# A list schedule over the recorded program in place of a scheduler with priorities, in a hybrid encoder block on one core

## The chip, the cores and the metric

The kernel runs on one core of one Trainium2 chip. The metric is device time in microseconds of one execution. A core has TensorE (matrix products into PSUM), VectorE (DVE), ScalarE (ACT), GpSimd (POOL) and SyncE (SP, which here only issues transfers). Each engine has a queue of its own that it works through in order; between engines there are semaphores, so an instruction at the head of a queue holds up everything behind it until what it needs is there.

## The reference, cut to what matters

One layer of an encoder: 512 positions, model width 1024, everything in float32.

```python
h = rmsnorm(x); proj = h @ w_in                      # 1024 -> 768 + 256 + 32 + 3*512
c_q, c_kv, k_pe, u_h = split(proj)
q = rmsnorm(c_q) @ w_uq; kv = rmsnorm(c_kv) @ w_ukv  # 8 heads, q/k of 64 + 32 (rotary), v of 64
q, k = rope(rmsnorm(q)), rope(rmsnorm([k_nope, k_pe]))
y_attn = softmax(q k^T / sqrt(96)) v                 # bidirectional
x0, x1, vh = split(dwconv3(u_h))
y_hyena = x0 * (fftconv(x1 * vh, filters) + bias * x1 * vh)   # filters: three sine layers, a decay
x = x + [rmsnorm(y_attn), rmsnorm(y_hyena)] @ w_out
up = dwconv3(rmsnorm(x) @ w_up); x = x + (silu(g) * u) @ w_down   # 2 x 2816
x = x + sigmoid(x @ w_gate) * rmsnorm(p @ w_ple)
```

## The kernel before, in words

Activations lie transposed: channels on the 128 partitions, the 512 positions along the free dimension. A float32 product is made of three products of rounded parts: every operand is split into a high part (a copy on ScalarE) and a low part (a subtraction on VectorE), and mms (L173, matmuls at L176) runs high x high, high x low, low x high. Weights come as 128 x 1024 tiles in one stream of their own order: next_w (L166) keeps the loads three tiles ahead, and wload (L137) makes a transfer into wr on SP, the high part wh on ScalarE (L142) and the low part wl on VectorE (L143), for half of many tiles by a transfer from GpSimd's queue that adds (L145, L146).

The stages in order of time are: the loads of x and its squares (accx, accy); the input projections, 21 tiles of 24 matmuls each (in_gemm, L313), of which the first three are the kv latents and the rotary key; the norm's scale R1 (rms_bcast, L218, and rsqrt, L203: a logarithm, an exponential and a Newton step on ScalarE and VectorE) with which every product is multiplied as it leaves PSUM (L509, L621); between them the Hyena filters (filter_task, three sine layers at L370 to L377) and the transforms of the Hyena input, as matmuls with a table dft; the products of the spectra on VectorE (L589 to L599) and their sums, split into Y (L610); the keys (wk) and the six query tiles in the order UQ; head sums of the squares by matmuls with sel, whose eight rows are copied by ScalarE (rows, L667), turned by four tiny transposes (turn_rows, L231) and made into scales (rms_cols); the list TAIL, in which inverse transforms (E, O), values (V), first scores (S) and a gate (G) stand; the attention, 8 heads of four row blocks each (scores, softmax, turn, weigh, finish), with the other gates (products at L833 to L835, square and sum at L841 and L842, then a split) and the Hyena part of the output product (hyena_out, residual add at L929) mixed in; the attention part of the output product; 44 up tiles with their convolution (conv, L536 to L543), silu and gate; the down product; the embedding; the last gate with sigmoid and the store.

PSUM has eight banks in two rings of four, mm (psm) and ax (psx). Temporaries of the first stages are ten rotating tiles (tmp, NTMP), x tiles are eight, weights three high, three low and two raw.

What sets the order of the work is this. TensorE's order is written out by hand: its matmuls are issued as the program text makes them. Side work of TensorE (filter, transforms, key, query scale) is written as generators that are woven into the projections by a clock: advance(cost) adds the cost in us of the matmuls just made, and spawn(task, delay) puts a task's next piece at clock + delay; these delays are the constants D_SIN, D_FILT, D_RMS and so on. All other engines are put in order by the framework's scheduler at build time: it goes by priorities, which follow the program order, changed by offsets in the table PRI and by high_priority blocks, and by its own estimate of the times. rope, ident and the dft tables are loaded by SP and GpSimd in the middle of this; the GpSimd ones are held behind the statistics by issue_after. L651 fixes one place at which ScalarE's exponential table is loaded.

Pools of tiles open and close with ExitStack: ft (first stages) closes at L893 before the attention's pools at and ap open in its place, and at, ap, hp and gp close before fp, the pool of the feed-forward stage.

## Time and profile before

| | |
|---|---|
| three runs, median (lowest to highest) | 759.44 us (757.58 to 759.54) |
| the profiled execution, its own time | 757.62 us |
| its span, from first to last instruction | 755.8 us |
| mean granted TensorE clock | 0.991 |
| TensorE busy | 723.0 us (96%), 3254 matmuls recorded |
| VectorE, ScalarE, GpSimd busy | 504.8, 373.1, 151.7 us |
| read from memory | 77.00 MB, 105 GB/s over the span |

A row of a timeline has the start in us, the busy time in us, the engine, the line, the operation, the tiles out<-in, the form and the count; in brackets stands the idle time of the engine before it and what ended it. A row of a wait says which instruction of which engine waited for which: us in total, times, longest. A granted clock below 1.00 in a stretch means that TensorE was throttled for part of it. A line can be a helper's: L176 is every matmul of mms, L131, L132, L134 and L135 are the two halves of split.

### The profile page before, as it was taken

What the parts mean: (1) busy time and instruction counts of PE and PEld (TensorE: products, weight loads), DVE (VectorE), ACT (ScalarE), POOL (GpSimd) and SP (SyncE); (2) the same over time, 40 slices, a digit from 0 to 9 for tenths busy, and PEclk for the clock granted to TensorE, in tenths of its full rate; (3) what the DMA queues carried; (4) which work ended last, traced back from release to release, by engine and by line L of the source; (5) the groups of instructions that cost most, each with busy time, mean ns of one, the idle gap of its engine ahead of it and who ended that gap; (6) DMA issues with size and microseconds to landing.
All of it is one profiled execution on the core that took longest, in us unless ns stands there. A gap on an engine that the chain in (4) does not pass through costs nothing.

```text
span 755.8 us, 9037 instructions
## 1 busy us (share of the span) xinstructions
PE 723.0 (96%) x3254; PEld 582.7 (77%) x3254; DVE 504.8 (67%) x780; ACT 373.1 (49%) x575; POOL 151.7 (20%) x150
## 2 busy tenths in 40 slices
PE   6999999996997899999999999999999999999997
PEld 4767888874665777788888888888888888888886
DVE  6499988888779987885766566666665332233482
ACT  7465545467668896564534444444353222126340
POOL 2111101110126662130422222222122000005000
PEclk9999999997999999999999999999999999999999
DMA  8765744443636210533232323232323233323331
GB/s 279 239 153 128 191 128 91 106 94 77 147 91 170 71 25 19 126 103 106 83 113 84 112 84 112 83 104 92 106 89 92 82 109 101 98 90 127 111 112 56
DMA packets 30110, 82.83 MB, mean 110 GB/s; under 512 B 3913, under 2 KB 5257, under 8 KB 30066
## 3 DMA queue, kind: packets, MB, share of 16 engines
q1 hardware_dynamic: 24418, 71.62, 31.2%
q0 software_dynamic: 5392, 10.25, 7.2%
q10 hardware_dynamic: 256, 0.39, 0.2%
q8 instruction: 25, 0.41, 0.2%
q14 instruction: 19, 0.16, 0.1%
HBM read 77.00 MB, written 2.10 MB: 105 GB/s over the span
## 4 chain that ended last, share of the span: by engine, by line
PE 54%; DVE 0%; ACT 0%; DVEq 0%; issue 0%
PE mm L176 37%; PE ax L176 17%; PE ax L220 0%; DVE t L1127 0%; ACT t L1126 0%; DVEq L1294 0%; DVE t L1128 0%
## 5 line engine op out<-in xcount | busy, mean ns | idle before, releaser
L176 PE MATMUL mm<-a,wh 128*128 128x512 f32 (+1 forms) x928 | 288.8, 392 | 9.2 <-ACT wh L273 6.4
L176 PEld LDWEIGHTS mm<-a,wh 128*128 128x128 f32 x928 | 174.3, 190 | 51.2 <-issue 6.5
L143 DVE TENSOR_TENSOR wl<-wr,wh 128x1024 fp32r<-128x1024 f32 (+3 forms) x113 | 124.3, 1101 | 113.8 <-ACT wh L142 111.8
L142 ACT ACTIVATE wh<-wr 128x1024 fp32r<-128x1024 f32 (+1 forms) x113 | 116.5, 1031 | 158.0 <-PE mm L176 121.6
L176 PE MATMUL mm<-a,wl 128*128 128x512 f32 (+1 forms) x464 | 180.7, 389 | 0.0
L176 PE MATMUL ax<-a,wh 128*128 128x512 f32 x384 | 118.3, 389 | 0.0
L176 PEld LDWEIGHTS mm<-a,wl 128*128 128x128 f32 x464 | 88.1, 190 | 17.8 <-DVE wl L274 0.2
L176 PEld LDWEIGHTS ax<-a,wh 128*128 128x128 f32 x384 | 72.1, 188 | 14.9
L176 PE MATMUL mm<-g,wh 128*128 128x512 f32 x232 | 73.8, 400 | 1.7 <-ACT t L647 1.7
L176 PE MATMUL ax<-a,wl 128*128 128x512 f32 x192 | 74.7, 389 | 0.0
L1063 POOL TENSOR_TENSOR f<-f 128x512 f32<-128x512 f32 x22 | 28.7, 1303 | 169.2 <-DVE f L543 149.5
L176 PE MATMUL mm<-h,wh 128*128 128x512 f32 x192 | 59.0, 389 | 0.0
L176 PEld LDWEIGHTS mm<-g,wh 128*128 128x128 f32 x232 | 44.2, 192 | 13.7 <-ACT t L647 2.1
L176 PE MATMUL mm<-g,wl 128*128 128x512 f32 x116 | 46.1, 397 | 0.0
L176 PEld LDWEIGHTS ax<-a,wl 128*128 128x128 f32 x192 | 36.0, 188 | 7.6
L176 PEld LDWEIGHTS mm<-h,wh 128*128 128x128 f32 x192 | 36.0, 188 | 7.5
L1059 DVE TENSOR_TENSOR f<-mm,R 128x512 f32<-128x512 f32 x22 | 15.2, 691 | 33.7 <-PE mm L176 33.7
L176 PE MATMUL mm<-h,wl 128*128 128x512 f32 x96 | 37.3, 389 | 0.0
L1062 ACT ACTIVATE f<-f 128x512 f32<-128x512 f32 x22 | 13.9, 631 | 44.8 <-DVE f L543 44.8
L536 ACT ACTIVATE f<-f,par 128x512 f32<-128x512 f32 x44 | 35.5, 808 | 1.0 <-DVE f L1059 1.0
L543 DVE SCALAR_TENSOR_TENSOR f<-f,par 128x511 f32<-128x511 f32 x44 | 33.9, 771 | 1.4
L146 POOL DMA_DIRECT2D wl<-in_w_in_dram x16 | 13.9, 868 | 103.8 <-DVE wl L143 53.5
(312 smaller groups left out, 1015.1 us busy)
## 6 DMA issues: line engine op xcount, KB each, us to landing
wr<-in_w_up_dram SPq DMA_DIRECT2D x44, 512.0 KB, 3.5
wr<-in_w_in_dram SPq DMA_DIRECT2D x19, 512.0 KB, 3.9
wr<-in_w_down_dram SPq DMA_DIRECT2D x16, 512.0 KB, 3.5
x<-in_xT_dram SPq DMA_DIRECT2D x16, 256.0 KB, 4.2
wl<-in_w_in_dram POOLq DMA_DIRECT2D x16, 256.0 KB, 5.3
wr<-in_w_out_dram SPq DMA_DIRECT2D x8, 512.0 KB, 4.4
wr<-in_w_gate_dram SPq DMA_DIRECT2D x8, 512.0 KB, 3.6
wr<-in_w_down_dram SPq DMA_DIRECT2D x8, 384.0 KB, 3.1
```

What stands on the lines that cost most here:

```text
L142: S.activation(hi[:, :n], raw[:, :n], AF.Copy)
L143: V.tensor_tensor(lo[:, :cut], raw[:, :cut], f32(hi[:, :cut]), op=ALU.subtract)
L146: G.dma_start(lo[:, cut:n], src[:, cut:n], accum_op=ALU.add)
L176: last = PE.matmul(out, l, r, start=start and i == 0, stop=stop and i == n - 1)
L536: S.activation(c, z, AF.Identity, scale=pcol(w, 3 * m + 1), bias=pcol(b, m))
L543: V.scalar_tensor_tensor(c[:, 0 : T - 1], z[:, 1:T], pcol(w, 3 * m + 2), c[:, 0 : T - 1], op0=ALU.mult, op1=ALU.add)
L1059: V.tensor_tensor(z, ps_up.pop(m), R2, op=ALU.mult)
L1062: S.activation(cc[0], cc[0], AF.Silu)
L1063: G.tensor_tensor(cc[1], cc[0], cc[1], op=ALU.mult)
```

## The change

The body of the kernel is nearly unchanged, but its engines are now recorders. Every call (matmul, activation, transfer) becomes an Op in a Plan, with the tiles and boxes that it reads and writes. Tiles become PlannedTile, whose buffer is chosen by the planner. At the end plan.issue() puts all ops in sequence and only then emits them, each engine's in the order found. The framework orders nothing any more (engines=None), and all high_priority blocks, PRI offsets and the fixed place of the table load are gone (issue preloads the exponential table wherever the plan changes back to it).

The order is found as follows. TensorE's ops get a due time each, by adding up their durations in recorded order from 5.5 us. Every other op is due in time for the earliest of its successors: that one's due time less its own duration and latency, for a transfer also 2 us and its bytes. Successors are found through data only (overlapping boxes of a tile). Then time is played through: of each engine's ready ops the one that can start first is taken, and among those within 0.02 us of it the one due first. TensorE's ops can therefore leave the recorded order. Tiles of one tag take buffers in recorded order, when one is free. Ops before a pool change (close) are all placed before any op after it. The durations come from a cost function; all but TensorE's and SP's are stretched by 1.05, and an operation of VectorE or GpSimd with `port` is not placed beside one of the other.

Further edits: the delays of the side tasks are new, with query_scale at 18.5 instead of 6.5 and the sine layers at 2.0 instead of 8.0; UQ is now 5, 2, 4, 3, 0, 1; KLAG goes from 3 to 2 and NRH, the block at which the Hyena norm is made, from 10 to 15. Of the entries in ENG three take effect: the residual adds of hyena_out (xt, L929) go from VectorE to GpSimd; the scaled sum in the Hyena norm (vh) goes from VectorE to ScalarE; the squares in rms_cols (sc) do so too. QACT goes from 1 to 0, so head 0's four transfers in prep (L745, L746) are issued by SP instead of ScalarE. rope and ident are now recorded as behind the statistics too, which only the plan sees.

```diff
@@ -23,37 +23,37 @@
 T_IN = 5.1
 T_UQ = 3.9
 T_K = 1.3
-D_SIN = 8.0
-D_FILT = 9.5
-D_TR = 5.0
-D_HALF = 7.0
-D_RMS = 6.5
+D_SIN = 2.0
+D_FILT = 13.5
+D_TR = 1.0
+D_HALF = 8.5
+D_RMS = 18.5
 D_LAT = 0.0
-D_UU = 13.5
-D_UT = 5.0
+D_UU = 13.0
+D_UT = 1.0
 D_MUL = 3.5
-D_SPR = 2.0
+D_SPR = 6.0
 D_SQ = 13.0
 NTMP = 10
 D_LR = 7.0
-D_KC = 2.5
-D_RC = 1.5
+D_KC = 4.5
+D_RC = 2.5
 W0N = 512
 W0B = 2
 W1A = 3
 W1B = 4
-KLAG = 3.0
-NRH = 10
-D_FT = 8.5
+KLAG = 2.0
+NRH = 15
+D_FT = 11.5
 TAIL = 'E0 P E1 R O S0 S1 V0 V1 S2 S3 V2 G0 V3'
...
-QACT = 1
-UQ = (2, 0, 4, 3, 5, 1)
-D_KS = 5.0
-D_KR = 4.5
-D_TAIL = 15.5
+QACT = 0
+UQ = [5, 2, 4, 3, 0, 1]
+D_KS = 6.0
+D_KR = 5.0
+D_TAIL = 16.5
...
+MARGIN = 0.1
+AIM = 0.0
+STRETCH = {'V': 1.05, 'S': 1.05, 'G': 1.05, 'PE': 1.0, 'SP': 1.0}
...
+    def cost(self, op):
+        a, kw = op.args, op.kw
+        out = a[0]
+        n = 1
+        for k in out.shape[1:]:
+            n *= k
+        op.table, op.byte, op.lat, op.port = None, 0, 0.2, False
+        if op.fn == "dma_start":
+            op.byte = 4 * n * out.shape[0]
+            op.dur = 0.6 if op.eng == "G" else 0.45
+            op.lat = 0.0
+            return
+        if op.eng == "PE":
+            if op.fn == "transpose":
+                op.dur = 0.11 if a[1].shape[0] > 8 else 0.07
+            elif a[1].dtype == F32:
+                op.dur = max(0.222, 0.855 * n / T) if n > 8 else 0.222
+            else:
+                op.dur = (n + 32) / 2400.0
+            op.lat = 0.25
+        elif op.eng == "V":
+            if op.fn == "reduce_max":
+                op.dur = 0.6
+            elif op.fn in ("tensor_tensor", "stream_shuffle"):
+                op.dur = 0.07 + n / 960.0
+            elif op.fn == "reciprocal":
+                op.dur = 0.1
+            elif op.fn == "tensor_scalar" and not any(isinstance(v, View) for v in a[2:]) and not a[1].tile.tag.pool.psum:
+                op.dur = 0.08 + n / 1900.0
+            else:
+                op.dur = 0.12 + n / 960.0
+            op.lat = 0.22
+            ins = [v for v in list(a[1:]) + list(kw.values()) if isinstance(v, View) and v.shape[1] * len(v.shape) > 16]
+            op.port = n > 64 and len(ins) > 1 and not any(v.tile.tag.pool.psum for v in ins)
+        elif op.eng == "S":
+            op.dur = 0.09 + n / 1190.0
+            if isinstance(kw.get("scale"), View) or isinstance(kw.get("bias"), View):
+                op.dur += 0.06
+            if kw.get("accum_out") is not None:
+                op.dur += 0.15
+            op.lat = 0.24
+            op.table = TABLES.get(a[2])
+        elif op.eng == "G":
+            op.dur = 0.05 + (n / 780.0 if op.fn == "tensor_scalar" else n / 410.0)
+            op.port = n > 64 and op.fn != "memset"
+        else:
+            op.dur = 0.1
+
+    def order(self):
+        clock = 5.5
+        for op in self.ops:
+            if op.eng == "PE":
+                op.due = clock
+                clock += op.dur
+            else:
+                op.due = None
+            for p in op.preds:
+                p.succs.append(op)
+        for op in reversed(self.ops):
+            need = clock + 50.0 if op.due is None else op.due
+            for s in op.succs:
+                need = min(need, s.due - op.dur - op.lat - AIM - (2.0 + op.byte / 2.0e5 if op.byte else 0.0))
+            op.due = need
+        engines = {e: 0.0 for e in self.handles}
+        port = {"V": 0.0, "G": 0.0}
+        table, moved, done = "exp", 0.0, []
+        begun = 0
+        for seg in range(len(self.cuts) + 1):
+            last = self.cuts[seg] if seg < len(self.cuts) else len(self.ops)
+            ops = self.ops[begun:last]
+            begun = last
+            ready = {e: [] for e in engines}
+            for op in ops:
+                op.wait = sum(1 for p in op.preds if p.end is None)
+                op.est = max([p.end for p in op.preds if p.end is not None], default=0.0)
+                if not op.wait:
+                    ready[op.eng].append(op)
+            left = len(ops)
+            while left:
+                best = None
+                for e, cand in ready.items():
+                    now, fit = None, []
+                    for op in cand:
+                        t = max(op.est, engines[e])
+                        if op.port:
+                            t = max(t, port["G" if e == "V" else "V"])
+                        ok = True
+                        for tile, _, _ in op.acc:
+                            if tile.slot is None:
+                                tag = tile.tag
+                                if tag.tiles[tag.next] is not tile:
+                                    ok = False
+                                    break
+                                slots = [s for s in tag.open_slots() if s.free is not None]
+                                if not slots:
+                                    ok = False
+                                    break
+                                t = max(t, min(s.free for s in slots))
+                        if ok:
+                            fit.append((t, op))
+                    if not fit:
+                        continue
+                    now = min(t for t, _ in fit)
+                    t, op = min(((t, op) for t, op in fit if t <= now + 0.02), key=lambda x: (x[1].due, x[1].i))
+                    if best is None or t < best[0]:
+                        best = (t, op)
+                assert best is not None, "no operation fits"
+                t, op = best
+                for tile, _, _ in op.acc:
+                    if tile.slot is None:
+                        tag = tile.tag
+                        slot = min((s for s in tag.slots if s.free is not None), key=lambda s: s.free)
+                        slot.free, tile.slot = None, slot
+                        tag.next += 1
+                dur = op.dur * STRETCH[op.eng]
+                if op.table is not None and op.table != table:
+                    dur += 1.28
+                    table = op.table
+                engines[op.eng] = t + dur
+                op.end = t + dur + op.lat
+                if op.port:
+                    port[op.eng] = t + dur
+                if op.byte:
+                    rate = 1.0e5 if op.kw.get("accum_op") is not None else 2.7e5
+                    moved = max(moved, t + dur) + op.byte / (2.7e5)
+                    op.end = max(moved, t + dur + op.byte / rate) + 2.0
+                for tile in {x[0] for x in op.acc}:
+                    tile.left -= 1
+                    tile.end = max(tile.end, op.end)
+                    if not tile.left:
+                        tile.slot.free = tile.end
+                ready[op.eng].remove(op)
+                for s in op.succs:
+                    if s.seg == seg:
+                        s.wait -= 1
+                        s.est = max(s.est, op.end + (MARGIN if s.eng != op.eng else -op.lat))
+                        if not s.wait:
+                            ready[s.eng].append(s)
+                done.append((t, op))
+                left -= 1
+        self.done = done
+        return done
+
...
+            real = lambda v: v.real() if isinstance(v, View) else v
+            getattr(self.handles[op.eng], op.fn)(*[real(v) for v in op.args], **{k: real(v) for k, v in op.kw.items()})
...
-    V, S, G, PE, SP = nc.vector, nc.scalar, nc.gpsimd, nc.tensor, nc.sync
+    plan = Plan(tc, {"V": nc.vector, "S": nc.scalar, "G": nc.gpsimd, "PE": nc.tensor, "SP": nc.sync})
+    V, S, G, PE, SP = (plan.engine(k) for k in ("V", "S", "G", "PE", "SP"))
...
-    ctx.enter_context(tc.manual_schedule(engines={mybir.EngineType.PE}))
+    ctx.enter_context(tc.manual_schedule(engines=None))
...
-    SP.dma_start(rope, c_rope)
-    SP.dma_start(ident, c_id)
-    with tc.issue_after(gate_consts.ins):
+    plan.behind = gate_consts
+    if True:
+        SP.dma_start(rope, c_rope)
+        SP.dma_start(ident, c_id)
...
-    p0.close()
...
+    plan.close(ft)
...
+    plan.issue()
```

More of the change, by code (lines that the diff above doesn't have):

```diff
@@ new lines, with __init__, open_slots, view @@
+class Slot:
+    def __init__(self, pool, tag, n):
+        self.pool, self.tag, self.n = pool, tag, n
+        self.free = 0.0
+class Tag:
+    def __init__(self, pool, name, bufs):
+        self.pool, self.name, self.bufs = pool, name, bufs
+        self.tiles, self.next, self.slots = [], 0, None
+    def open_slots(self):
+        if self.slots is None:
+            self.slots = [Slot(self.pool, self, n) for n in range(min(self.bufs, len(self.tiles)))]
+        return self.slots
+class PlannedTile:
+    def __init__(self, tag, shape, dtype):
+        self.tag, self.shape, self.dtype = tag, tuple(shape), dtype
+        self.width = 1
+        for n in shape[1:]:
+            self.width *= n
+        self.slot, self.left, self.first, self.end, self.real = None, 0, None, 0.0, None
+        self.log = []
+    def view(self):
+        return View(self, np.arange(self.shape[0] * self.width, dtype=np.int32).reshape(self.shape), (), self.dtype)
@@ new lines, with __init__, __getattr__ @@
+class Op:
+    __slots__ = ("i", "eng", "fn", "args", "kw", "acc", "seg", "preds", "succs", "dur", "lat", "due", "wait", "est", "new", "end", "table", "byte", "port")
+class Recorder:
+    def __init__(self, plan, eng, handle):
+        self._plan, self._eng, self._handle = plan, eng, handle
+    def __getattr__(self, fn):
+        return lambda *args, **kw: self._plan.record(self._eng, fn, args, kw)
+TABLES = {AF.Ln: "exp", AF.Exp: "exp", AF.Sin: "sin", AF.Silu: "silu", AF.Sigmoid: "sigmoid"}
@@ L162, in ahead @@
         while len(ready) < min(i, len(stream)):
-            with tc.high_priority(offset=WPRI if len(ready) > 3 else 0):
+            with nullcontext():
                 ready.append(wload(*stream[len(ready)]))
@@ L506, in tile_encoder_block @@
         G.memset(f32(t8), 0.0)
+    plan.behind = None
     ckv = [xpool.tile([P, T], F32, tag="x", name="x") for _ in range(2)]
```

190 lines of the change are left out of this document (163 added, 27 removed).

## The prediction

> **What bounds the kernel now.** I read the page first (engines, slices, chain), then the waits of TensorE alone, then stretches of the span cut where those waits lie, then the timelines around the longest ones.
>
> ```profile
> span 755.8 us, 9037 instructions
> PE 723.0 (96%) x3254; PEld 582.7 (77%) x3254; DVE 504.8 (67%) x780; ACT 373.1 (49%) x575; POOL 151.7 (20%) x150
> PE   6999999996997899999999999999999999999997
> PE 54%; DVE 0%; ACT 0%; DVEq 0%; issue 0%
> ```
>
> TensorE is busy 723.0 of 755.8 us, and the chain that ended last is TensorE for 54% of the span, some 408 us back from its last matmul near 751 us. The change removes no matmul, so the whole stake is TensorE's idle time of 32.8 us and the time in which its clock is low. Stretches (span, busy time and count of PE, PEld, DVE, ACT, POOL, then the granted clock, DMA share, GB/s) place both:
>
> ```profile
> 0.00:6.40 6.40, 0.00 (x0) 0.00 (x0) 0.76 (x2) 3.15 (x5) 0.45 (x6) 1.00 0.55 172
> 33.00:35.00 2.00, 0.14 (x2) 0.07 (x1) 1.93 (x4) 0.15 (x1) 0.00 (x0) 1.00 0.89 230
> 35.00:39.40 4.40, 4.40 (x13) 3.46 (x14) 2.83 (x6) 3.71 (x6) 0.88 (x1) 0.61 0.51 109
> 39.40:57.00 17.60, 16.71 (x65) 11.52 (x64) 16.59 (x28) 10.80 (x15) 1.73 (x2) 1.00 0.59 146
> 57.00:160.00 103.00, 103.00 (x460) 84.37 (x458) 93.02 (x159) 49.27 (x75) 12.97 (x15) 1.00 0.54 129
> 160.00:175.80 15.80, 14.15 (x59) 9.65 (x58) 13.18 (x23) 12.06 (x20) 2.60 (x3) 1.00 0.45 88
> 175.80:182.00 6.20, 0.43 (x5) 0.32 (x4) 6.20 (x12) 5.21 (x9) 0.00 (x0) 0.79 0.27 86
> 182.00:189.60 7.60, 7.58 (x18) 4.39 (x18) 4.84 (x14) 5.19 (x11) 0.86 (x1) 0.50 0.11 23
> 189.60:228.00 38.40, 36.14 (x161) 25.38 (x160) 28.51 (x67) 25.89 (x55) 7.90 (x9) 1.00 0.50 122
> 228.00:313.00 85.00, 76.69 (x437) 62.31 (x438) 75.47 (x164) 64.85 (x130) 42.73 (x47) 1.00 0.31 77
> 313.00:751.10 438.10, 437.63 (x1946) 361.53 (x1944) 243.38 (x285) 175.31 (x226) 75.35 (x57) 1.00 0.32 99
> 751.10:755.80 4.70, 0.00 (x0) 0.00 (x0) 1.43 (x4) 0.66 (x2) 0.00 (x0) 1.00 0.17 56
> ```
>
> Two pieces are out of reach: the first 6.4 us (the first loads) and the last 4.7 us (last sigmoid, two products, store). From 313 to 751.1 us only 0.47 us is idle. The remaining 21.2 us, 20.7 of it in the rows shown, lies before 313 us. To it comes slow matmul time: 4.4 us at clock 0.61 loses 4.4 x 0.39 = 1.7 us, 7.6 us at 0.50 loses 3.8 us. The pool is 21.2 + 5.5 = 26.7 us. Second thing to see: VectorE is busy 16.59 + 93.02 + 13.18 + 6.20 + 4.84 + 28.51 = 162.3 of the 188.6 us from 39.4 to 228 (86%) and 75.47 of 85 (89%) after it, so it is nearly a second bound there.
>
> The waits of TensorE (us in total, times, longest):
>
> ```profile
> PE ax L231 <- ACT t L667: 6.5, 2, 5.8
> PE ax L176 <- DVE ptl L132: 3.2, 2, 2.9
> PE mm L176 <- DVE x L509: 1.9, 1, 1.9
> PE mm L176 <- ACT t L647: 1.7, 1, 1.7
> PE ax L370 <- ACT x L377: 0.9, 1, 0.9
> ```
>
> **The change part by part.** The sum is made against the profiled execution: 757.62 us, 1.8 us around its span. Its runs have the median 759.44.
>
> **(1) The stall at 175.8 us.** Four tiny transposes of the query's row sums (L231) stand in TensorE's fixed order before the copy that feeds them (L667) is made. ScalarE's queue holds that copy behind splits that each wait for VectorE:
>
> ```profile
> 171.08 1.02 PE L674 MATMUL ax<-accx,ones 128*8 128x512 f32 x2
> 182.01 0.59 PE L231 MATMUL ax<-ident,t 8*128 8x8 f32 x4 [5.79 <-ACT t L667]
> 179.65 0.63 ACT L131 ACTIVATE a<-t 128x512 fp32r<-128x512 f32 x1 [0.58 <-DVE t L610]
> 181.39 0.57 ACT L667 ACTIVATE t<-ax 8x512 f32<-8x512 f32 x1
> ```
>
> The sums were done at 172.1, the copy started at 181.4. After the change query_scale is recorded 18.5 us of TensorE cost behind the keys instead of 6.5, so some 12 us of query matmuls go ahead of it; the copy inherits an early due time from the transposes; and the planner lets a ready matmul overtake one whose operand is late. Best case 5.79 + 3.8 = 9.6 us. Late next are the key's own row sums, which go through the same copy, and Y, the spectra whose sixteen VectorE operations (L610, L132) fill that queue. VectorE has 13.18 + 6.20 + 4.84 of 29.6 us filled, that is 24.2; with 9.6 us closed only 20.0 us are left, so 4.2 us of its work must slide on, into 189.6 to 228, where it has 9.9 us free. I take 8.0 (range 2 to 9.6).
>
> **(2) The stall at 33 us.** The fifth projection needs a PSUM bank that L509 frees, which needs R1, the input norm's scale:
>
> ```profile
> 27.54 2.24 ACT L142 ACTIVATE wh<-wr 128x1024 fp32r<-128x1024 f32 x2 [7.96 <-DMA wr<-in_w_in_dram]
> 30.20 0.67 ACT L205 ACTIVATE R<-ax,eps 128x512 f32<-128x512 f32 x1
> 34.12 1.29 DVE L509 TENSOR_TENSOR x<-mm,R 128x512 f32<-128x512 f32 x2
> ```
>
> ScalarE waited 7.96 us for a weight with the logarithm of R1 queued behind it. An order by due times could start it ahead of the two splits (2.24 us) and recover 1.9 + 1.7 = 3.6 us. But due times run through data, not through PSUM banks: freeing a bank gives no urgency, and the two weight splits keep theirs. Between 0 and 3.6 I take half, 1.8. The row at 35 us shows clock 0.61 after an idle time of 1.86 us. The Trainium skill (TensorE: Matmul & The Clock Gate, "Why this matters for your kernels") says to avoid idle gaps over some 3 us, since a window of idle halves the clock; by that rule this stall would cost 1.9 and its cure half of that; the trace here goes against the rule, since the shorter gap already halved the clock.
>
> **(3) Two small stalls,** 0.9 (third row of the small filter network waits for its sine) and 1.7 (a bank waits for the square at L647): greedy order of TensorE should fill about half, 1.3 of 2.6 (0 to 2.6).
>
> **(4) 189.6 to 228,** 2.26 us idle. Here the softmax scale is a chain of small operations, and pulling the rest of the stretch together uncovers it. Against it: the plan closes at each pool change (L893), so all operations recorded before the attention precede all later ones on every engine. Gate 0's split, now run at 234.12 amid the attention, must come before the first probabilities; that is one VectorE operation of 0.76 us. Net 0.8 (-1 to 2.3).
>
> **(5) The attention, 228 to 313,** 8.3 us idle, VectorE at 89%. The longest stall follows one operation:
>
> ```profile
> 234.12 2.94 DVE L135 SCALAR_TENSOR_TENSOR a<-x,par,a 128x512 fp32r<-128x512 f32 x1
> 242.75 0.76 DVE L135 SCALAR_TENSOR_TENSOR a<-x,par,a 128x512 fp32r<-128x512 f32 x1
> 233.92 1.36 POOL L869 TENSOR_SCALAR pr<-pr,st 128x512 f32<-128x512 f32 x2
> 235.25 1.26 POOL L842 TENSOR_TENSOR x<-x,t 128x512 f32<-128x512 f32 x1
> 238.01 0.68 DVE L132 TENSOR_TENSOR ptl<-ax,pth 128x512 fp32r<-128x512 f32 x1
> 238.84 0.93 PE L176 MATMUL ax<-ks,qs 96*128 96x512 f32 x3 [2.93 <-DVE ptl L132]
> L929 DVE TENSOR_TENSOR x<-x,t x8: 679/682/693, 261.6 to 317.0; 128x512 f32<-128x512 f32 x8
> L208 DVE TENSOR_SCALAR t<-ax 128x512 f32<-128x512 f32 x1 | 0.7, 672 | 0.0
> ```
>
> The same split takes 0.76 us alone and 2.94 us while GpSimd runs three operations back to back (to 236.5): 2.2 us lost. The planner's cost keeps such a VectorE operation (two inputs in SBUF) from being placed while GpSimd is on the port, and does something else first. The residual add L929 (0.68 us) moves from VectorE to GpSimd, three of eight inside the attention: 2.0 us off VectorE. The Hyena norm's scaled sum (L208) moves to ScalarE, 0.7 us. Together VectorE sheds 2.2 + 2.0 + 0.7 = 4.9 us, of which TensorE can win what it waits for. On GpSimd the nearest row is 1.26 us (L842), 10.1 us for eight, under its 42.27 us of free time. This part speaks against itself, too. The Trainium skill (SBUF — State Buffer, "Who interferes with whom") says that a VectorE operation with two SBUF inputs and a GpSimd operation that reads SBUF exclude each other for a whole instruction; by it each moved add could block VectorE for up to 1.3 us where it took 0.7, and part 5 would lose about 2 us more; the 2.94 us row agrees with that rule. I take 2.5 won (-4 to 5).
>
> **(6) Edits costed at nothing.** QACT 0 moves head 0's four transfer issues from ScalarE to SP; ScalarE has 12.5 us free in 189.6 to 228 and gains about 2, SP may hold them behind a weight load. The queue of SP waited at most 5.9 us for such a thing:
>
> ```profile
> 185.32 0.52 ACTq L745 DMA_DIRECT2D qr<-g  x1
> SPq L745 <- DMA kr<-x: 5.9, 1, 5.9
> ```
>
> So 0, between -4 and +1. Rope and identity now count as behind the statistics in the plan, and SP still issues them when it has nothing more urgent. The small square in rms_cols swaps one short engine for another. The new UQ order, KLAG 2 and the other delays only change due times. From 313 us on TensorE is dense with VectorE at 243.38 of 438.10, so any sane order keeps it full; cover gone, each weight chain late by 1 us would cost 1 us.
>
> **(7) Misjudged durations.** The plan prices the convolution's ScalarE operation (L536) at 0.09 + 512/1190 + 0.06, stretched by 1.05, 0.61 us, and the row below says 0.81. In the dense 57 to 160 us VectorE is 90% busy, and where the plan is short its fixed queues stall TensorE anew. Bound 0 to 10, taken 2.0 lost.
>
> ```profile
> L536 ACT ACTIVATE f<-f,par 128x512 f32<-128x512 f32 x44 | 35.5, 808 | 1.0 <-DVE f L1059 1.0
> ```
>
> Sum: 8.0 + 1.8 + 1.3 + 0.8 + 2.5 - 2.0 = 12.4 us. 757.62 - 12.4 = 745.2 against the profiled execution; the median stood 1.8 above it, of which I add about half: **746**.
>
> **The rivals.**
>
> *Everything closes (chance 0.15).* The planner fills nearly the whole pool, since hyena_out and the values are matmuls ready to slip into gaps. For it: greedy order has no gap while a matmul is ready. Against: banks open in recorded order, and VectorE's 89%. With 22 of 26.7: about 736.
>
> *VectorE is the bound (0.12).* Parts 1 to 4 only move idle time on: VectorE's 162.3 us and their latencies do not shrink, and TensorE meets the same backlog a little later. For it: 86 to 90% over 190 us, with a stall whose releaser itself waits for VectorE. Gains of 1 to 2 us: 757, no change.
>
> *Banks are not urgent (0.15, slower).* The place is 57 to 160 us, where TensorE now never waits. Products with R1 (L621) free the four mm banks, but their due time comes from transforms far behind, so weight splits and filter work with nearer dues go first. It decides once a product waits longer than the three projections that the other banks cover, each 24 matmuls of 5.44 us together as in this row, 16.3 us:
>
> ```profile
> 358.22 5.44 PE mm L176 x24
> ```
>
> The price: twelve projections late by 1.2 us each, 14.4, and two dips of the clock as at 35 us, 3.4; less 8 us of gains elsewhere: 757.62 + 9.8 = 767. Against: VectorE has 10 us free there, and takes whatever is ready.
>
> *The attention pays (0.08, slower).* First ready, first served puts gate and residual work ahead of the probabilities: 32 blocks late by 0.4 us each, 12.8, against 9.9 us won in parts 1 to 4 less part 7's 2.0: 757.62 + 4.9 = 762.5.
>
> **How the numbers follow.** My forecast has 0.50, and its own range is 738 to 753. About 0.3% (2.3 us) is what a measurement can tell from no change. Faster: 0.50 + 0.15 and a little of the unchanged case, 0.66; slower: 0.15 + 0.08 less a little, 0.22; the same 0.12. The range takes in the second rival and most of the first, and the milder end of the slow cases: 733 to 763.
>
> **What would show it.** Right in (1): no wait of L231 over 1 us near 180 us and no clock of 0.50 there; the attention starts near 217 instead of 228. (2): no dip of the clock near 35 us. (5): no L135 over 1.5 us, and VectorE below 89% or the stretch below 83 us. (7): idle TensorE inside the projections, released by L621 or a weight split, would prove the third rival; an attention stretch over 90 us the fourth. If 175 to 228 us has not shrunk by 5 us, the forecast is wrong.

## The result and the profile after

The kernel after took 739.77 us in the median, beside 758.75 us for the kernel before in the same comparison: a ratio of 0.975, with a 95% interval from 0.9731 to 0.9769. That is 19.0 us less. The time lies inside the range of 733 to 763 and 6.2 us under the forecast of 746. The profiled execution took 739.88 us with a span of 738.1, 17.7 us below the span before; the prediction's sum, made for that execution, was 12.4. Of the four executions of the kernel after, one ran at a mean granted clock of 0.849 and took 808.28 us; the other three lie between 739.51 and 739.88, and only such undisturbed ones are compared here.

The page of the kernel after (the columns are those shown of before: busy time, share, instructions, then tenths of a slice):

```profile
span 738.1 us, 9053 instructions
PE 718.2 (97%) x3254; PEld 580.8 (79%) x3254; DVE 509.6 (69%) x768; ACT 370.8 (50%) x579; POOL 177.1 (24%) x158
PE   6999999998989999999999999999999999999997
```

TensorE does the same 3254 matmuls in 4.8 us less busy time (718.2 against 723.0; 3.8 of it is the half clock, which lost 5.5 us before and loses 1.7 now) and is idle for 19.9 us instead of 32.8. GpSimd is busy 25.4 us more. All recorded calls now leave from one line, the emitting line of the plan (L441), so instructions are told apart by their tiles alone.

The longest waits of TensorE after (us in total, times, longest):

```profile
PE mm L441 <- ACT wh L441: 6.8, 2, 5.7
PE mm L441 <- ACT t L441: 3.5, 1, 3.5
PE ax L441 <- DVE ptl L441: 1.5, 1, 1.5
```

The first row is the start of the kernel (5.7) and one piece of 1.16 us soon after it. The 5.8 us wait for the copied row sums is gone, and a new wait of 3.5 us stands in its place.

To compare stages I cut both spans at the same five events: TensorE's first matmul, the last of the projections, the first turned probability of the attention, the row sums of the attention's output and the last matmul. First the kernel before, then the kernel after (columns as in the prediction's stretches):

```profile
0.00:6.42 6.42, 0.00 (x1) 0.01 (x1) 0.78 (x2) 3.17 (x5) 0.45 (x6) 1.00 0.56 173
6.42:154.20 147.78, 144.54 (x607) 114.58 (x608) 125.24 (x207) 77.22 (x114) 20.93 (x26) 0.99 0.62 164
154.20:224.00 69.80, 61.26 (x249) 42.05 (x248) 54.98 (x111) 47.84 (x92) 10.59 (x12) 0.93 0.41 97
224.00:300.50 76.50, 67.03 (x404) 54.49 (x402) 68.16 (x158) 62.15 (x130) 42.61 (x48) 1.00 0.30 75
300.50:751.10 450.60, 450.13 (x1998) 371.55 (x1998) 254.23 (x302) 182.02 (x235) 77.11 (x59) 1.00 0.32 99
```

```profile
0.00:5.68 5.68, 0.00 (x0) 0.00 (x0) 0.54 (x1) 3.21 (x5) 0.45 (x6) 1.00 0.62 182
5.68:150.10 144.42, 142.87 (x611) 113.95 (x612) 128.26 (x212) 77.42 (x116) 21.54 (x26) 1.00 0.62 166
150.10:212.70 62.60, 59.06 (x245) 40.52 (x244) 51.38 (x102) 47.07 (x92) 8.13 (x10) 0.97 0.53 129
212.70:285.80 73.10, 69.78 (x420) 57.83 (x419) 64.50 (x157) 64.01 (x134) 50.57 (x54) 1.00 0.25 66
285.80:733.30 447.50, 446.41 (x1983) 368.52 (x1981) 263.27 (x295) 178.43 (x233) 96.41 (x64) 1.00 0.32 99
```

| stage | before | after | difference |
|---|---|---|---|
| until TensorE starts | 6.42 | 5.68 | -0.74 |
| projections, filters, keys | 147.78 | 144.42 | -3.36 |
| queries, up to the attention | 69.80 | 62.60 | -7.20 |
| attention | 76.50 | 73.10 | -3.40 |
| all the rest | 450.60 | 447.50 | -3.10 |
| behind the last matmul | 4.70 | 4.80 | +0.1 |

The last two stages are to be read together. The attention holds 16 matmuls more than before (420 against 404) and the rest 15 fewer. Those were pulled forward into gaps: the idle time of the attention fell from 9.47 us (76.50 less 67.03) to 3.32 (73.10 less 69.78), that is by 6.15 us. Of these, 3.40 show as a shorter attention; the other 2.75 were filled with matmuls (69.78 less 67.03), and the rest is 3.10 shorter.

Stretches of the kernel after, at the places that the prediction named:

```profile
33.00:57.00 24.00, 24.00 (x98) 17.84 (x98) 22.42 (x38) 15.22 (x21) 4.45 (x5) 1.00 0.68 176
174.70:178.30 3.60, 0.06 (x2) 0.02 (x1) 2.00 (x5) 3.60 (x7) 0.86 (x1) 1.00 0.69 150
178.30:182.70 4.40, 4.40 (x14) 3.16 (x15) 3.43 (x9) 4.34 (x10) 0.00 (x0) 0.61 0.72 175
182.70:212.70 30.00, 30.00 (x127) 19.29 (x126) 21.95 (x51) 20.46 (x45) 2.95 (x4) 1.00 0.46 122
```

From 33 to 57 us nothing is idle any more and the clock is 1.00. At 174.7 us TensorE stands for 3.54 us and then has a mean clock of 0.61 over 4.4 us (1.7 us lost). The timeline there, TensorE's row first (the wait in brackets), then ScalarE's:

```profile
178.28 0.73 PE L441 MATMUL mm<-g,wh 128*128 128x512 f32 x2 [3.54 <-ACT t L441]
180.35 0.59 PE L441 MATMUL ax<-ident,t 8*128 8x8 f32 x4
174.55 1.06 ACT L441 ACTIVATE wh<-wr 128x1024 fp32r<-128x1024 f32 x1 [1.59 <-PE mm L441]
177.55 0.67 ACT L441 ACTIVATE t<-mm,par 128x512 f32<-128x512 f32 x1
```

A query tile's first matmul needs a bank of the mm ring. The ScalarE operation that empties it (177.55) stands behind a weight's high part (174.55), which itself had to wait 1.59 us for a matmul to let go of its buffer, and behind four further operations. The four tiny transposes at 180.35 are those of the key's row sums; they start without any idle time, and so do the query's, from 190.62 us on.

The splits of the gates in the attention, of which one took 2.94 us before, are all short now (rows of the stretch from 212.7 to 285.8 us):

```profile
L441 DVE SCALAR_TENSOR_TENSOR a<-x,par,a 128x512 fp32r<-128x512 f32 x4 | 3.0, 740 | 0.6 <-ACT a L441 0.6
```

### The profile page after: what moved, and what is told of

It is laid out like the page before. It is cut to its first block, busy times and chain, and to the rows that moved or that the text cites. A ratio compares the mean times of both kernels' runs of the same rounds, so it can differ in the third digit from the quotient of the medians.

```text
span 738.1 us, 9053 instructions
## 1 busy us (share of the span) xinstructions
PE 718.2 (97%) x3254; PEld 580.8 (79%) x3254; DVE 509.6 (69%) x768; ACT 370.8 (50%) x579; POOL 177.1 (24%) x158
## 4 chain that ended last, share of the span: by engine, by line
PE 55%; DVE 1%; issue 0%; ACT 0%; DVEq 0%
PE mm L441 38%; PE ax L441 18%; DVE a L441 0%; DVE pl L441 0%; DVE t L441 0%; ACT t L441 0%; DVEq L1650 0%; DVE x L441 0%
## 5 line engine op out<-in xcount | busy, mean ns | idle before, releaser
L441 PE MATMUL mm<-a,wh 128*128 128x512 f32 (+1 forms) x928 | 310.4, 390 | 6.9 <-ACT wh L441 6.8
L441 ACT ACTIVATE wh<-wr 128x1024 fp32r<-128x1024 f32 (+2 forms) x117 | 119.1, 1020 | 256.3 <-PE mm L441 192.5
L441 PEld LDWEIGHTS mm<-a,wh 128*128 128x128 f32 x928 | 173.3, 189 | 45.2 <-ACT wh L441 7.6
L441 PE MATMUL mm<-a,wl 128*128 128x512 f32 (+1 forms) x464 | 171.9, 391 | 0.0
L441 DVE TENSOR_TENSOR wl<-wr,wh 128x1024 fp32r<-128x1024 f32 (+3 forms) x117 | 121.3, 1040 | 68.9 <-ACT wh L441 68.7
L441 PE MATMUL ax<-a,wh 128*128 128x512 f32 x384 | 147.1, 389 | 0.0
L441 PEld LDWEIGHTS mm<-a,wl 128*128 128x128 f32 x464 | 87.4, 189 | 19.1 <-DVE t L441 0.8
L441 DVE SCALAR_TENSOR_TENSOR f<-f,par,f 128x511 f32<-128x511 f32 x88 | 85.9, 980 | 2.7 <-ACT f L441 1.2
L441 PEld LDWEIGHTS ax<-a,wh 128*128 128x128 f32 x384 | 72.0, 188 | 14.9
L441 PE MATMUL mm<-g,wh 128*128 128x512 f32 x232 | 80.1, 397 | 3.5 <-ACT t L441 3.5
L441 PE MATMUL ax<-a,wl 128*128 128x512 f32 x192 | 74.7, 389 | 0.0
L441 PE MATMUL mm<-h,wh 128*128 128x512 f32 x192 | 65.9, 389 | 0.0
L441 POOL TENSOR_TENSOR f<-f,f 128x512 f32<-128x512 f32 x22 | 29.3, 1331 | 143.4 <-DVE f L441 125.2
L441 PEld LDWEIGHTS mm<-g,wh 128*128 128x128 f32 x232 | 43.9, 190 | 14.7 <-ACT t L441 4.0
L441 DVE TENSOR_TENSOR f<-mm,R 128x512 f32<-128x512 f32 x22 | 15.2, 691 | 46.4 <-PE mm L441 46.3
L441 POOL TENSOR_TENSOR acc<-acc,t 128x512 f32<-128x512 f32 x13 | 18.8, 1448 | 113.8 <-ACT t L441 103.1
L441 PE MATMUL mm<-g,wl 128*128 128x512 f32 x116 | 45.2, 395 | 0.0
L441 PEld LDWEIGHTS ax<-a,wl 128*128 128x128 f32 x192 | 36.0, 188 | 7.5
L441 PEld LDWEIGHTS mm<-h,wh 128*128 128x128 f32 x192 | 36.0, 188 | 7.5
L441 POOL DMA_DIRECT2D wl<-in_w_in_dram x16 | 13.9, 871 | 102.4 <-DVE wl L441 40.0
L441 ACT ACTIVATE f<-f,par 128x512 f32<-128x512 f32 x44 | 35.3, 806 | 5.2 <-DVE f L441 5.2
L441 PE MATMUL mm<-h,wl 128*128 128x512 f32 x96 | 37.4, 389 | 0.0
```

Source lines behind the costliest of these rows:

```text
L441: getattr(self.handles[op.eng], op.fn)(*[real(v) for v in op.args], **{k: real(v) for k, v in op.kw.items()})
```

## The experiments

The kernels were timed in three groups, each beside the kernel before (760.64, 758.28 and 759.73 us): the first four, the next four, the last four. Ratios are to the kernel before of the same group, with 95% intervals.

**1. The planner with all the old numbers.** Every constant of the change (delays, UQ, KLAG, NRH, the entries of ENG, QACT) goes back; the list schedule stays.

```diff
-D_SIN = 2.0
-D_FILT = 13.5
...
-D_RMS = 18.5
+D_SIN = 8.0
+D_FILT = 9.5
...
+D_RMS = 6.5
...
-QACT = 0
-UQ = [5, 2, 4, 3, 0, 1]
+QACT = 1
+UQ = (2, 0, 4, 3, 5, 1)
```

> The planner as changed, with every constant of the kernel before (delays, UQ, KLAG, NRH, the engines of xt, vh and sc, QACT). Theory A, the schedule itself gains and the constants only fit it: 744 to 750 us, over half of the 19 us. Rival B, the constants carry the gain (query_scale 12 us later above all): 755 to 760, and the wait of the tiny transposes stays over 4 us.

Measured: 746.93 us, 0.9823 (0.9794 to 0.9853). TensorE's two longest waits behind the first matmul, and the one at the tiny transposes:

```profile
PE mm L441 <- ACT t L441: 2.4, 1, 2.4
PE ax L441 <- POOL a L441: 1.8, 1, 1.8
PE ax L441 <- ACT t L441: 1.0, 1, 1.0
```

The schedule alone brings 13.7 us (760.64 less 746.93); the new numbers bring 5.3 us as the rest of the 19.0, or 7.0 by the spans of the profiled executions (745.1 to 738.1); run 1 and the kernel after were not timed side by side. The tiny transposes wait 1.0 us, although query_scale is still recorded 6.5 us behind the keys: the delay was not needed to cure the stall at 175.8.

**2. The new numbers under the old scheduler.**

Here the diff is to the kernel before, and all constants of the change are taken over.

```diff
-D_SIN = 8.0
-D_FILT = 9.5
+D_SIN = 2.0
+D_FILT = 13.5
...
-D_RMS = 6.5
+D_RMS = 18.5
...
```

> The kernel before with its own scheduler and TensorE's order by hand, and every constant of the changed kernel. Theory A: the delays mean something else there (a sine layer every 2 us of TensorE cost), so it does not gain: 757 to 770. Rival B: 740 to 747.

Measured: 772.05 us, 1.0143 (1.0109 to 1.0178), slower than before. Three of its waits:

```profile
PE ax L370 <- ACT x L377: 8.7, 1, 8.7
PE ax L231 <- ACT t L667: 4.6, 2, 3.9
PE mm L176 <- DVE x L509: 1.8, 1, 1.8
```

The numbers are no gain in themselves. With sine layers 2.0 us apart, a filter matmul in its fixed place waits 8.7 us for its sine; the wait for L509 at 33 us is untouched. With query_scale later, the query's tiny transposes (212.87 us) wait no more; the 3.9 us are now those of the key's row sums (199.22 us), which the prediction had named as late next.

**3. and 4. The planner with TensorE kept in recorded order,** with the old numbers (3) and with the new (4). One TensorE operation at a time is allowed to be a candidate:

```diff
         begun = 0
+        line = [op for op in self.ops if op.eng == "PE"][::-1]
...
                     for op in cand:
+                        if e == "PE" and op is not line[-1]:
+                            continue
...
                 ready[op.eng].remove(op)
+                if op.eng == "PE":
+                    line.pop()
```

> The planner with the constants of before, and TensorE's matmuls kept in the order in which they are recorded: only the other queues are planned. Theory C, the gain is TensorE's freedom to let ready matmuls overtake: 755 to 762, no better than before. Against C, the order of ScalarE and VectorE makes the gain: within 3 us of the run with the old constants and TensorE free.

> The changed kernel with TensorE kept in recorded order. Theory C: the new delays stall a fixed order (sine layers 2 us apart whose chain takes longer), 760 to 775. Against C: 740 to 745.

Measured: 770.58 us, 1.0131 (1.0099 to 1.0163), and 765.99 us, 1.0069 (1.0045 to 1.0094): both slower than before. But both hold a stall that neither kernel compared has, so the numbers can't be taken for the price of the fixed order. Run 4, timeline of TensorE, ScalarE and SP's queue:

```profile
235.53 1.23 PE L446 MATMUL mm<-pth,g 128*128 128x256 f32 x4 [10.34 <-ACT pth L446]
233.33 0.63 ACT L446 ACTIVATE ks<-kr 96x512 fp32r<-96x512 f32 x1 [9.87 <-DMA kr<-x]
221.45 1.10 SPq L446 DMA_DIRECT2D kr<-x  x2
```

ScalarE waits 9.87 us for a head's keys to arrive, and TensorE waits for ScalarE. SP issues two transfers of keys, at 221.45 and at 226.22 us. The first has waited itself, and all that stands behind it in SP's queue came late with it:

```profile
SPq L446 <- PE ax L446: 13.0, 2, 12.5
```

The matmul that SP waited for shares no data with this transfer. Its tile, the keys of head 3, lies in the pool ap, which opens in memory that a closed pool left. The plan follows its own pools, but not which memory lies under them. That reading is tested in runs 9 to 11.

Up to that stall run 3 can be used. The wait for the bank at 33 us is 0.40 us there (the waits of run 3, whose only such row is this):

```profile
PE mm L446 <- DVE x L446: 0.4, 1, 0.4
```

TensorE's order is as recorded, so ScalarE's and VectorE's planned order alone cured the stall at 33 us. It did not cure the one at 175.8. The query's tiny transposes in run 3:

```profile
177.81 0.59 PE L446 MATMUL ax<-ident,t 8*128 8x8 f32 x4 [5.51 <-ACT t L446]
```

It takes either the later query_scale or TensorE's freedom. The first turned probability of the attention, which lies ahead of the late transfer, comes at 226.2 us in run 3 and at 217.2 in run 1: up to there the freedom is worth 9.0 us with the old numbers, too, and the planned side queues without it gain nothing over the kernel before (224.0).

**5. The residual adds of hyena_out back on VectorE.**

```diff
-ENG = {..., 'xt': 'G', ...}
+ENG = {..., 'xt': 'V', ...}
```

> The changed kernel with the eight residual adds (xt) back on VectorE. If the move to GpSimd is part of the gain, as the prediction's part 5 has it (2 us off VectorE): 741 to 743. If the port makes the move worthless: 739 to 740.

Measured: 741.06 us, 0.9778 (0.9756 to 0.98). The interval overlaps the one of the kernel after (0.9731 to 0.9769). The median lies at the low edge of the first case. The move is worth 1.3 us by the medians and 2.1 by the ratios, and is not told apart from nothing.

**6. The planner without its bookkeeping of the port.**

```diff
-                        if op.port:
+                        if False:
                             t = max(t, port["G" if e == "V" else "V"])
```

> The changed kernel whose planner no longer keeps VectorE operations with two SBUF inputs from being placed beside GpSimd operations. If that bookkeeping made part 5's gain (the 2.94 us split): 742 to 746, with VectorE operations of two inputs over 1.5 us in the attention again. Else within 1 us of 739.8.

Measured: 752.63 us, 0.9916 (0.9894 to 0.9939). That is slower than either case expected. It too holds the transfer that waits for a matmul (a stall of TensorE of 8.79 us that begins at 218.3); run 11 repeats it without that.

**7. A due time for the emptying of a PSUM bank.** Every operation that reads a PSUM tile, other than TensorE's, is also due in time for the first matmul of the tile that takes its bank next:

```diff
...
+                        for op in users[tag.tiles[n]]:
+                            if op.eng != "PE" and op.i < tile.first.i:
+                                op.heirs.append(tile.first)
...
-            for s in op.succs:
+            for s in op.succs + op.heirs:
                 need = min(need, s.due - op.dur - op.lat - AIM - (2.0 + op.byte / 2.0e5 if op.byte else 0.0))
```

> The changed kernel whose due times also run from a PSUM tile's readers to the first matmul of the tile that comes four places later in its ring. If the 3.5 us stall at 174.7 us is a bank freed late for lack of urgency (the third rival's mechanism, at the query tiles instead of the projections): that stall under 1 us and 735 to 738. If it is ScalarE's queue blocked for another reason: 739 to 741.

Measured: 739.88 us, 0.9748 (0.9729 to 0.9767): the time of the kernel after and of the second case. Yet the stage changed much as the first one says. TensorE's row at the old stall, then a turned probability and the row sums, which close the attention:

```profile
174.92 0.72 PE L453 MATMUL mm<-g,wh 128*128 128x512 f32 x2 [1.50 <-ACT t L453]
208.03 0.60 PE L453 MATMUL ax<-ident,a 128*128 128x128 f32 x4
281.66 1.02 PE L453 MATMUL ax<-acc,ones 128*128 128x512 f32 x2
```

The stall shrank from 3.54 to 1.50 us, not under 1 us as expected: the weight's high part still goes ahead of the emptying operation and still waits 1.59 us for its buffer. The half clock behind the stall is gone, the attention starts 4.7 us earlier (208.0 against 212.7) and ends 4.1 earlier (281.7 against 285.8). All of that is given back within 20 us. The timeline of run 7 behind the attention, and the stretch that follows it:

```profile
292.86 4.27 DVE L453 SCALAR_TENSOR_TENSOR a<-yp,par,a 128x512 fp32r<-128x512 f32 x2 [0.29 <-ACT a L453]
293.13 2.78 POOL L453 TENSOR_TENSOR x<-x,t 128x512 f32<-128x512 f32 x2
296.52 0.62 PE L453 MATMUL mm<-a,wh 128*128 128x512 f32 x1 [2.11 <-DVE a L453]
```

```profile
296.60:300.30 3.70, 3.70 (x10) 2.89 (x11) 2.90 (x5) 0.00 (x0) 1.27 (x1) 0.54 0.41 93
```

Two splits on VectorE take 4.27 us together, 3.61 and 0.74 with a short overlap (one alone took 0.74 us a moment before), beside two residual adds on GpSimd. TensorE waits 2.11 us for them and then runs 3.70 us at 0.54, another 1.7 us: 3.8 of the 4.1 us. So most of the stall was the bank's late release, and the cure works at its place, but on this path the same kind of collision that part 5 of the prediction described took its place. A version with both cures was not run.

**8. A dearer price for the convolution's ScalarE operation,** for part 7 of the prediction:

```diff
+            if isinstance(kw.get("scale"), View) and isinstance(kw.get("bias"), View):
+                op.dur += 0.13
```

> The changed kernel whose planner prices a ScalarE operation with a column scale and a column bias 0.13 us dearer (0.75 us stretched, measured 0.81). If part 7's loss is real (2 us from prices that are short): 737 to 739. If not: 739 to 741.

Measured: 742.07 us, 0.9789 (0.9769 to 0.9809). The time lies above both cases: nothing is gained by the truer price, and the kernel is, if anything, slower.

**9. The control for the memory: the pools ap and at opened in the other order,** and nothing else.

```diff
+    ap_ = plan.pool("ap", 1, reuse_waits="tile")
     at = plan.pool("at", 1, reuse_waits="tile")
...
-    ap_ = plan.pool("ap", 1, reuse_waits="tile")
```

> The changed kernel with the attention's two pools opened in the other order, which only moves their tiles in memory: the control for the next two. In it, as in the changed kernel, the transfer of head 3's keys waits for no matmul. 739 to 741.

Measured: 739.59 us, 0.9744 (0.971 to 0.9777), the same as the kernel after.

**10. Run 4 with that swap: TensorE in recorded order, without the late transfer.**

```diff
+        line = [op for op in self.ops if op.eng == "PE"][::-1]
...
+                        if e == "PE" and op is not line[-1]:
+                            continue
...
+    ap_ = plan.pool("ap", 1, reuse_waits="tile")
     at = plan.pool("at", 1, reuse_waits="tile")
...
-    ap_ = plan.pool("ap", 1, reuse_waits="tile")
```

> TensorE kept in recorded order (new constants), with the pools swapped so that the transfer of head 3's keys no longer waits for the last reader of the memory beneath it, which cost the first run of this kind 10.3 us and 13.7 us of half clock. If TensorE's freedom carries the gain: 754 or more still. If that first run was slow only for the wait: 741 to 748.

Measured: 753.23 us (750.18 to 758.21 in ten runs), 0.9917 (0.9889 to 0.9945). Against run 4 the swap takes away 12.8 us by the medians (765.99 to 753.23) and 11.5 by the ratios, as the two were timed in different groups. It took nothing from the kernel after: the late transfer came from the memory under the pool. Against run 9 the fixed order costs 13.6 us. The time is just under the 754 that the expectation asked for, and so the reading is a little less sharp than it was put. Where it goes (waits of run 10, then its stretch at 47 us):

```profile
PE mm L446 <- DVE ptl L446: 5.6, 11, 0.8
PE ax L446 <- ACT x L446: 4.0, 1, 4.0
PE ax L446 <- DVE g L446: 2.8, 1, 2.8
PE ax L446 <- ACT t L446: 2.0, 2, 1.3
```

```profile
46.80:75.00 28.20, 21.37 (x67) 14.79 (x67) 24.70 (x42) 12.58 (x18) 1.73 (x2) 0.82 0.39 101
```

TensorE is idle 6.83 us there and at a mean clock of 0.82, while it waits for sines (x) and filter pieces (g) with projections standing behind them; the projections end at 162.1 instead of 149.1 in run 9. Of these 13.0 us, 9.5 are left at the first turned probability (221.3 against 211.8). With the old numbers the same difference was 9.0 us (runs 3 and 1), at other places; delays made for a fixed order under the plan were not tried. Of the tiny transposes, the key's wait 1.3 us here and the query's not at all, with TensorE's order fixed but query_scale 12 us later.

**11. Run 6 with the swap: no bookkeeping of the port, without the late transfer.**

```diff
-                        if op.port:
+                        if False:
...
+    ap_ = plan.pool("ap", 1, reuse_waits="tile")
     at = plan.pool("at", 1, reuse_waits="tile")
...
-    ap_ = plan.pool("ap", 1, reuse_waits="tile")
```

> The port left out of the plan, with the pools swapped in the same way. If the bookkeeping of the port is worth something: 742 to 747, with operations of VectorE stretched in the attention. If the first run lost its 13 us to the transfer alone: 738 to 741.

Measured: 743.02 us, 0.978 (0.9752 to 0.9807). The bookkeeping is worth 3.4 us by the medians (743.02 less 739.59); the intervals of the two ratios overlap, but the times do not (738.99 to 741.30 in run 9, 741.95 to 743.65 in run 11). VectorE's row in the attention, an operation that takes 0.67 us in the kernel after, stretched beside three of GpSimd; then what TensorE waited:

```profile
252.56 2.25 DVE L441 SCALAR_TENSOR_TENSOR R<-t,R 128x512 f32<-128x512 f32 x1
```

```profile
PE ax L441 <- DVE ptl L441: 2.7, 2, 1.5
```

**12. The planner with due times by position:** of what can start first, the operation recorded first is taken. (In the kernel after, TensorE's due times are not quite that already: an early need of a successor moves them forward, too.)

```diff
         engines = {e: 0.0 for e in self.handles}
+        for op in self.ops:
+            op.due = op.i
```

> The changed kernel whose due times are replaced by the position in the recorded program, on all engines (TensorE's was that already). If due times matter, as parts 1 and 2 have it (the row copy and the norm's scale get urgency from what needs them): 745 to 755. If ready first, served first does it all: 739 to 742.

Measured: 750.82 us, 0.9879 (0.9849 to 0.9909). The due times are worth 11 us (750.82 less 739.59), or 9.8 by the spans (747.0 against 737.2 in run 9): 2.2 before the attention, 5.8 in it and 1.8 behind it. From the first turned probability at 214.00 us to the row sums it takes 78.9 us, where the kernel after takes 73.1. Its two rows:

```profile
PE ax L443 <- DVE ptl L443: 4.9, 5, 1.9
```

```profile
292.86 1.02 PE L443 MATMUL ax<-acc,ones 128*128 128x512 f32 x2
```

At the two places where parts 1 and 2 of the prediction count on due times, they are not needed: without them the key's and the query's tiny transposes (182.98 and 191.98 us) start without a wait for their rows, and from 33 to 57 us TensorE is busy 24.00 of 24.00 us.

## Why the prediction was right, and where it was not

The forecast case came, and more of it than taken. That the sum came out short by only 5.3 us (12.4 against the 17.7 of the profiled executions) owes something to luck: parts 1 and 5 missed by some 3.6 us each in opposite ways, and part 2 came for another reason than the due times that it names. Part by part:

**(1) The stall at 175.8: the mechanism held, the size did not, since a new wait took part of it.** The wait for L667 is gone. The half clock, whose absence was asked for as well, is not: TensorE runs at 0.50 from 179.25 to 182.67 us, behind the new wait. Three reasons were given. Two of them would each do alone: with the old delay and TensorE free the wait is 1.0 us (run 1), with the late query_scale and TensorE fixed the query's transposes do not wait (run 10); with neither it is 5.51 (run 3). The third, the early due time of the copy, is not needed (run 12). "Late next" was put down to the key's row sums and to Y. The key's row sums came under the old scheduler (run 2, 3.9 us) and in a fixed order (run 10, 1.3), but in the kernel after it was a bank: 3.54 us and 1.7 of clock, a term that the sum does not have here. So the place won 9.6 - 5.2 = 4.4 us, where 8.0 were taken. The first turned probability comes 11.3 us earlier (212.7 instead of 224.0); the prediction, whose own mark for the attention is 228, asked for 11.

**(2) The stall at 33 us: the gain came, half of it was given away, and the reason was another.** All of the 3.6 us came, 1.8 were taken. The doubt (banks have no urgency) did not bite here, because the planned order of ScalarE and VectorE put R1 early enough by itself: run 3 has 0.40 us left with TensorE in its old order, while run 2, with the new numbers alone, keeps 1.8. But due times did not do it: run 12 has none and is as dense there. What is left, by exclusion, is the rule that the operation which can start first goes first.

**(3) and (4).** Both small stalls are gone, 2.6 us for 1.3. From 182.7 us to the attention TensorE is busy 30.00 of 30.00 us; with the gap of 1.51 us at 215.6, just behind that, the 0.8 taken is about right (2.26 less 1.51).

**(5) The attention is the term that was mis-sized most.** 6.15 us of idle time went, taken were 2.5, and the upper bound was 5. That bound added up what VectorE sheds (2.2 + 2.0 + 0.7), and left out that TensorE may bring other matmuls in while VectorE is late: 16 came in. The order weighs more than the shedding: the order by due times is worth 5.8 us in this stretch alone (run 12, 78.9 against 73.1), the port's bookkeeping 3.4 in the whole kernel (run 11), the residual adds 1.3 to 2.1, within the noise (run 5). VectorE is still busy 88% of the stage (64.50 of 73.10), against 89% before (68.16 of 76.50). The case against the part, with the rule of the Trainium skill on the shared port ("SBUF — State Buffer", "Who interferes with whom"), did not come true inside the attention: the four splits there take 740 ns in the mean. Just behind it the kernel after has such a collision as well, a split of 3.65 us at 303.45 beside a moved residual add, for which TensorE did not wait; in run 7 one at 292.86 cost TensorE 3.8 us.

**(6)** No idle time in the kernel after points at these edits; none was run by itself. (SP's longest wait at L745 before was 6.5 us, for qs of GpSimd; 5.9 was the one for kr alone.)

**(7) The 2.0 us lost to misjudged prices did not come.** A dearer price gave nothing (run 8). From 33 us to the end of the projections at 150.1 nothing is idle. What was lost was lost to the bank at 174.7.

**The rivals.** *VectorE is the bound* fell: the 88% stand, and the idle time went all the same. *The attention pays* fell: the stage is 3.4 us shorter. (Its price takes part 7's 2.0 us off twice: 12.8 less 9.9 makes 760.5, not 762.5.) *Banks are not urgent* had its mechanism right and its place and count wrong: not twelve projections but one query tile, once, 3.5 us and a dip; run 7 shows that giving banks a due time shrinks it to 1.50 us and takes the dip away. *Everything closes* (736) lies nearer to the time than the forecast does, 3.8 us off against 6.2, though its chance was 0.15: 17.7 of the 26.7 us of the pool went.

**Whose gain it is.** TensorE's freedom to let ready matmuls overtake is worth 13.6 us with the new delays (run 10 against 9), the due times 11 (run 12), the new numbers 5 to 7 (run 1), the port 3.4 (run 11). They overlap and do not add up to the 19.0. The new numbers without the schedule cost 11.4 us (run 2, 772.05 less 760.64).

**What stays open:** a small piece of run 7, 0.3 us; why the planner, which does keep such pairs apart in its own clock, let them meet at 292.86; what a fixed order would cost with delays of its own; which of the single new numbers brings the 5 to 7 us, and whether a part of that is a wait of SP for a matmul that run 1 holds in the attention (8.5 us, with no long wait of TensorE behind it).

## What to carry to other kernels

Where a fixed order of matmuls waits for other engines, let a ready matmul overtake a late one: here that took the waits away with old delays and with new, while delays that fit the free order were a loss in the fixed one (runs 2 and 10). When a plan orders all queues by due times, look for what its graph does not hold: here the bank that a tile needs next, and the memory under a pool that was closed. A cure at one place is worth what the next place leaves of it, so look for the give-back within the next 20 us before you believe a profile's local win.

## What the runs showed of the hardware that was not expected

**A short gap can halve the clock, and a longer one need not.** Run 7 has a gap of 2.11 us and behind it 3.70 us at 0.54 (rows above); before the change 1.86 us did it, as the prediction showed, while a longer gap of 2.93 us at 235.9 in the kernel before did not. So it is not the length of a gap alone that decides. The Trainium skill ("TensorE: Matmul & The Clock Gate", "Why this matters for your kernels") gives the bound as gaps of some 3 us and a window of idle time; by that bound the gaps of 2.11 and 1.86 us would have been free, and the measurements differ.

The traces show what does decide. Cut at its edges, the half clock (0.50) lasted 3.41 us in these cases and in the kernel after. Now count time in steps of that same length from such an edge, back and forth. The kernel before ahead of its dip, in it, and at the longer gap; then run 7 ahead of its dip and in it:

```profile
32.57:35.98 3.41, 1.55 (x8) 0.99 (x7) 3.25 (x5) 1.20 (x3) 0.00 (x0) 1.00 0.91 220
35.98:39.40 3.42, 3.42 (x10) 2.65 (x9) 1.85 (x5) 2.73 (x5) 0.88 (x1) 0.50 0.39 91
233.96:237.37 3.41, 1.95 (x15) 1.53 (x13) 3.41 (x4) 2.75 (x5) 2.56 (x3) 1.00 1.00 254
237.37:240.78 3.41, 1.94 (x12) 1.68 (x13) 3.41 (x11) 1.93 (x4) 1.33 (x2) 1.00 0.56 132
293.34:296.75 3.41, 1.30 (x6) 0.79 (x5) 3.41 (x2) 0.10 (x1) 2.57 (x3) 1.00 0.47 77
296.75:300.16 3.41, 3.41 (x9) 2.64 (x9) 2.61 (x5) 0.00 (x0) 1.15 (x1) 0.50 0.40 84
```

The short gaps fall into one step, which is left with 1.55 and 1.30 us of matmuls; the longer one is split over two steps, with 1.95 and 1.94. In all fourteen traces, counted in this way, each step at full clock with up to 1.72 us of matmuls was followed by half clock (26 of them), of four with 1.76 or 1.77 one was, and none that had more. So in these traces a step that is idle for about half of its 3.41 us costs 1.7 us more at the least, and where a gap falls counts as much as its length.

**VectorE beside GpSimd.** A split of 0.74 us took 3.61 us in run 7 and 3.65 in the kernel after (at 303.45) beside two operations of GpSimd, more than the 2.94 us of the prediction. In both cases the split began some 0.3 us ahead of GpSimd's first operation, while GpSimd was still issuing a transfer, and yet it ended behind the second. In the kernel after, the convolution's VectorE operations with the same two kinds of input take 980 ns in the mean of 88:

```profile
L441 DVE SCALAR_TENSOR_TENSOR f<-f,par,f 128x511 f32<-128x511 f32 x88 | 85.9, 980 | 2.7 <-ACT f L441 1.2
```

Before, the two groups of 44 (L537 and L543) took 752 and 771. It is the same collision: laid beside GpSimd's rows of the same trace, the 22 of the 88 that overlap an operation of GpSimd take 1.67 us in the mean, and none of the other 66 takes over 0.76. An operation with one of its inputs in PSUM (ptl<-ax,pth) takes 0.68 us with and without GpSimd beside it. The plan's bookkeeping, which forbids such pairs in the plan's own clock, does not keep them apart on the chip here. It costs nothing: TensorE is busy for 446.41 of the 447.50 us behind the attention.

**The memory of a reopened pool can hold up a transfer** for some 12.5 us behind a matmul that shares no data with it (run 4). By the medians that was 12.8 us of the whole kernel's time there and 9.6 in the pair of runs 6 and 11 (752.63 less 743.02); by the ratios it was 11.5 and 10.3.
